# Hybrid attention layer: score banks, look-ahead and small work in the differential heads

## The chip, the cores and the metric

The kernel runs on one core of one Trainium2 chip. The metric is the device time of one execution in microseconds (us). In the profile PE is TensorE (PEld its weight loads), DVE is VectorE, ACT is ScalarE, POOL is GpSimd, and SP is the queue that issues nearly all DMAs. L12 is line 12 of the kernel before; lines of the changed kernel are named as such.

## The reference

One decoder layer over 2048 tokens of width 1024. A pre-normed projection feeds eight stick-breaking heads of 64 and four differential heads (two 64-wide query and key maps each, values of 128). One output projection and a SwiGLU FFN follow. The change is in the differential heads:

```python
for start in range(0, S, Q_BLOCK):                      # S = 2048, Q_BLOCK = 128
    end = start + Q_BLOCK
    s = einsum('bhcqd,bhckd->bhcqk', q[:, :, :, start:end], k[:, :, :, :end]) * scale
    causal = arange(end)[None, :] <= arange(start, end)[:, None]
    p = softmax(where(causal, s, -inf), axis=-1)
    a = p[:, :, 0] - lam * p[:, :, 1]
    outs.append(einsum('bhqk,bhkd->bhqd', a, v[:, :, :end]))
```

Each head's output is RMS-normed afterwards. Queries and keys are normed and rotated (rope) before.

## The kernel before

The work is staged: norm and transposes of x; groups g = 0 to 3, pairs of stick-breaking heads; groups 4 to 7, one differential head each; the second part of the output projection; the FFN. Numbers are kept as a high and a low 16-bit half, so most products are three matmuls.

**Units.** A differential head has 16 query tiles i of 128 queries, with L = 128 (i + 1) columns of scores. `unit_diff` (L887) handles one map m and one chunk j of at most 1024 columns, so a tile has two units up to i = 7 and four from i = 8 on (n = 2 chunks), in the order m = 1, then m = 0. A head has 48 units. A unit has three parts:

- `scores` (L893): score matmuls into a place in PSUM, two per 512 columns, and the mask on the diagonal.
- `front` (L908): VectorE takes the row maximum of the scores (the helper `big`, so the trace shows L178), and for the second chunk joins it to the first one's (L919).
- `main` (L921): ScalarE makes the bias from the joined maximum (L925, only for chunk 0) and the exponential into SBUF with its row sum (L931). A two-chunk tile's first exponential thus needs both chunks' maxima.

**Clock.** Units are issued one by one. `clock.at(d, fn)` puts follow-up work d units later. After the last unit of a tile come `coefs` (sums joined at L950, reciprocal L951, factor L952), per chunk `mix` (VectorE, p0 + c p1), `high` (a float16 copy, on ScalarE at L974 for two chunks, on VectorE at L976 for one, then a DMA transpose at L327), `low` (the rest, L985 on GpSimd or VectorE through `big`), then `values` (matmuls with the transposed halves), `copy` (L1009, L1011), `power`, `store_high` (L1024), `store` (L1029). The transposed halves lie in a ring of eight.

**The loop** (from L1233) does for unit n: due evacuations; the maxima of unit n + 1; due small work; `main` of n; further due work; `look_ahead(n)`, which issues scores up to unit n + 2; then projection work (`fill_next`) as long as TensorE's count of columns is behind a goal. Since every engine takes its instructions in order, this order is the schedule. PSUM has eight banks of 512 columns; in the differential heads banks 0 to 5 are three fixed places of 1024 columns for scores, whatever a unit's width, and the last two serve projections and values (`places`, `place`).

**Projection.** `project_diff` (L593) makes q, k and v of 512 tokens as fill: `evac_v` (L641) writes v's halves on VectorE (L643, L644), twice in each of the 16 projections; `high` (L698) casts the rotated q on VectorE (L703) and k on ScalarE (L704).

Of the kernel before, what the change touches and what calls it, by code (L numbers as in the profile page):

```python
# [12 lines left out]
ALU = mybir.AluOpType  # L13
# [51 lines left out]
def hybrid_layer_kernel(  # L65
# [159 lines left out]
    with ExitStack() as actx:  # L225
# [28 lines left out]


# [343 lines left out]
        def project_diff(c, g):  # L599
# [19 lines left out]
            for j in range(4):  # L619
                yield from bank_totals()  # L620
                ps = pj_tile("pj")
                part(j, 0, ps[:, 0:128])
                yield
                part(j, 1, ps[:, 128:256])

                def evac(j=j, ps=ps):
                    nc.scalar.activation(
                        st[:, :, j], ps.rearrange("p (t m d) -> p t m d", t=2, m=2),
                        AF.Copy, scale=OUT_SC)

                clock.at(1, evac, "mid")
                yield END
                if j % 2 == 0:
                    continue
                yield from bank_totals()
                ps = pj_tile("pj").rearrange("p (j n) -> p j n", j=2)
                part(j - 1, 2, ps[:, 0])
                yield
                part(j, 2, ps[:, 1])

                def evac_v(j=j, ps=ps):  # L641
                    vh, vl = v[:, j - 1:j + 1, 0, :], v[:, j - 1:j + 1, 1, :]
                    nc.vector.tensor_scalar(vh, ps, OUT_SC, None, ALU.mult)  # L643
                    nc.vector.scalar_tensor_tensor(vl, ps, OUT_SC, vh, ALU.mult, ALU.subtract)  # L644

                clock.at(1, evac_v, "mid")
                yield END
# [51 lines left out]
            def high():  # L699
                n2 = r["rt"].bitcast(F16)  # L700
                r["n"] = n2[:, 0:1024], n2[:, 1024:2048]
                r["nk"], r["nq"] = (halves(a) for a in r["n"])
                nc.vector.tensor_copy(r["nq"][:, :, :, 0, :], xq)  # L703
                nc.scalar.copy(r["nk"][:, :, :, 0, :], xk)  # L704
# [56 lines left out]
        def unit_sb(g, s, c, a, cx, step):  # L761
# [114 lines left out]
            return scores, None, main, W, 3 * W + 3 * W + (384 if diag else 0)  # L876
# [9 lines left out]
        def unit_diff(g, i, m, j, cx):  # L886
# [6 lines left out]
            def scores():  # L893
# [3 lines left out]
                z = u["z"] = place("z", 1024)  # L897
# [10 lines left out]
            def front():  # L908

                if m == 1 and j == 0:  # L910
                    cx["mx"] = small("mx", 4, bufs=3)
                    cx["nb"] = small("nb", 4, bufs=3)
                    cx["su"] = small("su", 4, bufs=3)
                    cx["cf"] = small("cf", 4, bufs=8)
                mx = cx["mx"]
                jj = 2 * j + m
                big(nc.vector.reduce_max, mx[:, jj:jj + 1], u["z"][:, 0:e - b], axis=AX.X)
                if j > 0:
                    nc.vector.tensor_max(mx[:, m:m + 1], mx[:, jj:jj + 1], mx[:, m:m + 1])  # L919

            def main():  # L921
                mx, nb, su = cx["mx"], cx["nb"], cx["su"]
                jj = 2 * j + m
                if j == 0:
                    nc.scalar.activation(nb[:, m:m + 1], mx[:, m:m + 1], AF.Identity,  # L925
                                         scale=nds_sc, bias=lnk)
# [7 lines left out]
                if m == 0 and j == n - 1:  # L934
# [5 lines left out]
                    clock.at(7 + n, values, "mid")  # L940
                    clock.at(8 + n, copy, "")
                    clock.at(9 + n, power)
                    clock.at(10 + n, store_high, "hi")
                    clock.at(11 + n, store, "")

            def coefs():
                su, cf = cx["su"], cx["cf"]
                steps = []
                if n == 2:
                    steps.append(lambda: nc.vector.tensor_add(su[:, 0:2], su[:, 0:2], su[:, 2:4]))  # L950
                steps += [lambda: nc.vector.reciprocal(cf[:, 0:1], su[:, 1:2]),  # L951
                          lambda: nc.vector.tensor_scalar(cf[:, 1:2], cf[:, 0:1], su[:, 0:1], nlam,  # L952
                                                          ALU.mult, ALU.mult)]

                def eps():
                    nc.gpsimd.tensor_scalar(cf[:, 2:3], su[:, 0:1], su[:, 0:1], scl[g][:, 2:3],
                                            ALU.mult, ALU.mult)
# [10 lines left out]
            def high(jc):  # L968
# [4 lines left out]
                if n == 2:  # L973
                    nc.scalar.copy(wh, p0)  # L974
                else:
                    nc.vector.tensor_copy(wh, p0)  # L976
# [49 lines left out]
            def store():  # L1026
# [8 lines left out]
                2 * (e - b) + (3 * L if m == 0 and j == n - 1 else 0))  # L1035
# [158 lines left out]
        for g in range(NG):  # L1194
# [7 lines left out]
            for n, (scores, front, main, w, _) in enumerate(us):  # L1202
                done += w
                plan.append((g, scores, front, main, work * min(1, done / tot),
                             PROJ * min(1, max(0, n - 2) / 11 if g == NG - 1 else (n + 1) / first)))
# [27 lines left out]
        for n, (g, scores, front, main, goal, due) in enumerate(plan):  # L1233
# [6 lines left out]
            if front is not None and (n == 0 or plan[n - 1][0] != g):  # L1240
                front()
            if n + 1 < len(plan) and plan[n + 1][0] == g and plan[n + 1][2] is not None:
                plan[n + 1][2]()
# [6 lines left out]
            look_ahead(n)  # L1250
            if g == NG - 1 and since == 18:
# [519 lines left out]
```

## Time and profile before

| | |
|---|---|
| median of 3 runs | 2860.58 us (2860.14 to 2867.91) |
| the profiled execution | 2863.87 us, its span 2862.1 us |
| mean granted TensorE clock | 0.955 |
| exponentials of the differential heads (L931) | 192, from 753.8 to 1425.0 us |

The page gives the busy time of each engine over the span, then groups of instructions by line, with count, busy time, mean time of one and the idle time just before them with what ended it. A view by windows gives the busy time of each engine in chosen stretches; the view of waits adds up who waited for whom. "psum" is the one tile that holds all of PSUM.

### The profile page before, as it was taken

To read this page: it belongs to the slowest core of one execution; us is meant where nothing else is said; L and a number is where in the kernel's file an instruction comes from. 1 tells how busy PE (TensorE), PEld (TensorE's weight loads), DVE (VectorE), ACT (ScalarE), POOL (GpSimd) and SP (SyncE) were. 2 spreads that over 40 slices of the span, in tenths; PEclk is the share of its full clock that TensorE was granted. 3 is DMA by queue.
4 is the path that set the end of the run, shared out by engine and by line. 5 is a ranking of instruction groups with operands and counts; after the bars stand their busy time and mean duration, and the time that the engine had idled before them with its cause. 6 is when DMAs were issued, how large, how long until landed. Compare 5 with 4: busy or idle time off the path is not lost.

```text
span 2862.1 us, 50497 instructions
## 1 busy us (share of the span) xinstructions
PE 2532.1 (88%) x19626; PEld 1466.2 (51%) x19626; DVE 2325.4 (81%) x3609; ACT 1513.6 (53%) x2523; POOL 1463.8 (51%) x1131
## 2 busy tenths in 40 slices
PE   6978888887786887877997998999999999999999
PEld 4534445455675676665853444444444444444444
DVE  7898999888888888998739689989777767776776
ACT  5778788876555655555515444444443433343332
POOL 2454545547667676674214656655444444444442
PEclk8989999998898998988999999999999999999999
DMA  4576877866554555667766221221217421112111
GB/s 160 93 144 120 144 140 139 139 130 122 103 93 89 99 104 105 130 123 165 172 169 140 89 100 67 81 78 60 89 45 148 155 96 45 45 44 89 45 45 74
DMA packets 734096, 301.49 MB, mean 105 GB/s; under 512 B 618656, under 2 KB 713120, under 8 KB 733856
## 3 DMA queue, kind: packets, MB, share of 16 engines
q1 hardware_dynamic: 733712, 298.23, 46.3%
q8 instruction: 153, 2.51, 0.4%
q14 instruction: 87, 0.71, 0.1%
q0 software_dynamic: 144, 0.03, 0.0%
HBM read 127.27 MB, written 28.31 MB: 54 GB/s over the span
## 4 chain that ended last, share of the span: by engine, by line
PE 44%; DVE 20%; POOL 6%; issue 5%; ACT 5%; DMA 4%; SPq 1%; DVEq 0%; POOLq 0%; ACTq 0%
PE pw L167 34%; PE psum L167 10%; DVE fs L1379 2%; DMA wt<-wh 2%; DVE acc_a L1636 2%; DVE mx L178 2%; DVE pp L178 1%; DVE hh L1423 1%; DVE pp L807 1%; DVE wh L836 1%; DMA q<-rt 1%; DVE wmx L105 1%; DVE rt L683 1%; POOL sc L1553 1%; POOL qss L108 1%
## 5 line engine op out<-in xcount | busy, mean ns | idle before, releaser
L167 PE MATMUL pw<-t,fs 128*128 128x512 f16 x3696 | 808.3, 381 | 17.2 <-issue 11.7
L167 PEld LDWEIGHTS <-fs 128*128 128x128 f16 x3696 | 360.6, 98 | 455.9 <-issue 18.4
L818 POOL TENSOR_TENSOR pp<-pp 128x1024 f32<-128x1024 f32 (+1 forms) x160 | 325.0, 2031 | 319.4 <-DVE pp L815 141.2
L167 PE MATMUL pw<-acc_b,at 128*128 128x512 f16 x2112 | 463.3, 379 | 18.1 <-DVE cg L1561 11.7
L167 PE MATMUL psum<-k,q 64*128 64x512 f16 (+4 forms) x1600 | 288.6, 378 | 161.3 <-ACT pp L931 80.8
L167 PE MATMUL psum<-ws,h_hi 128*128 128x128 f16 x4096 | 380.2, 225 | 20.1 <-ACT psum L1011 10.6
L167 PE MATMUL psum<-ws,h_lo 128*128 128x128 f16 x2048 | 369.2, 225 | 0.0
L167 PEld LDWEIGHTS <-h_hi 128*128 128x128 f16 x4096 | 329.9, 101 | 49.2 <-issue 37.7
L167 PEld LDWEIGHTS <-at 128*128 128x128 f16 x2112 | 205.6, 98 | 267.8 <-issue 22.6
L1564 POOL TENSOR_TENSOR cg<-cg,cu 128x512 f32<-128x512 f32 x88 | 112.4, 1278 | 371.4 <-ACT cg L1563 337.3
L1636 DVE SCALAR_TENSOR_TENSOR acc_a<-pw,isd,acc_a 128x512 f32<-128x512 f32 x352 | 248.9, 744 | 54.5 <-PE pw L167 54.1
L1378 ACT ACTIVATE fs<-acc_b,fst 128x512 f16<-128x512 f32 x264 | 176.1, 714 | 216.6 <-POOL acc_b L1367 143.3
L1379 DVE SCALAR_TENSOR_TENSOR fs<-acc_b,fst,fs 128x512 f16<-128x512 f32 x264 | 248.6, 982 | 31.6 <-ACT fs L1378 31.5
L1553 POOL TENSOR_TENSOR sc<-sc 128x512 f32<-128x512 f32 x132 | 220.0, 1682 | 91.3 <-ACT sc L1547 91.3
L807 DVE TENSOR_TENSOR_SCAN pp<-pp,psum 128x256 f32<-128x256 f32 (+1 forms) x320 | 195.8, 652 | 58.7 <-ACT psum L804 57.8
L167 PEld LDWEIGHTS <-q 64*128 64x128 f16 (+1 forms) x1600 | 94.9, 99 | 271.7 <-issue 114.3
L1547 ACT COPY sc<-pw 128x512 f32<-128x512 f32 x176 | 100.3, 581 | 217.6 <-PE pw L167 191.3
L167 PEld LDWEIGHTS <-h_lo 128*128 128x128 f16 x2048 | 207.3, 101 | 0.0
L836 DVE TENSOR_TENSOR wh<-pp,wh 128x1024 f16<-128x1024 f32 (+1 forms) x160 | 205.0, 1281 | 1.1 <-DMA wt<-wh 1.1
L931 ACT ACTIVATE pp<-psum,nb,ds_sc 128x1024 f32<-128x1024 f32 (+4 forms) x192 | 183.0, 954 | 21.8 <-DVE pp L178 8.5
L178 DVE TENSOR_REDUCE mx<-psum 128x1 f32<-128x1024 f32 (+4 forms) x192 | 173.6, 905 | 19.9 <-PE psum L167 19.1
L802 ACT ACTIVATE pp<-psum,gsc 128x1024 f32<-128x1024 f32 (+1 forms) x160 | 164.8, 1030 | 38.2 <-PE psum L167 34.4
(215 smaller groups left out, 4503.6 us busy)
## 6 DMA issues: line engine op xcount, KB each, us to landing
acc_b<-in_w_gate_dram SPq DMA_DIRECT2D x22, 1024.0 KB, 5.3
acc_b<-in_w_up_dram SPq DMA_DIRECT2D x22, 1024.0 KB, 7.6
acc_b<-in_w_down_dram SPq DMA_DIRECT2D x22, 1024.0 KB, 9.5
raw<-in_w_in_dram SPq DMA_DIRECT2D x24, 512.0 KB, 4.5
pp<-in_x_dram SPq DMA_DIRECT2D x16, 512.0 KB, 5.2
wt<-wh SPq DMA_TRANSPOSE x512, 3.2
raw<-in_w_o_dram SPq DMA_DIRECT2D x16, 512.0 KB, 4.1
mt<-mix_d SPq DMA_DIRECT2D x32, 256.0 KB, 3.1
```

The source lines that it names most:

```text
L167: nc.tensor.matmul(ps, lhsT=lhsT, rhs=rhs, start=start, stop=stop)
L178: fn(*a, **k)
L802: nc.scalar.activation(be, z[:, :, 0:W], AF.Sigmoid, scale=sc[:, 0:1])
L807: nc.vector.tensor_tensor_scan(ga, ga, z[:, h, P:W][:, ::-1], 2.0 ** 14 if diag else cx[a][:, h, 0:1], ALU.mult, ALU.mult)
L818: nc.gpsimd.tensor_mul(b4, b4, gp[:, :, 1:P + 1].rearrange("p h (r n) -> p h r n", r=1).to_broadcast([128, 2, 2, P]))
L836: nc.vector.tensor_sub(wl[:, 0:n], b2, u["wh"][:, 0:n])
L931: nc.scalar.activation(pt, u["z"][:, 0:e - b], AF.Exp, scale=ds_sc, bias=nb[:, m:m + 1], accum_out=su[:, jj:jj + 1])
L1378: nc.scalar.activation(w[:, m, 0:4], src, AF.Copy, scale=sw)
L1379: nc.vector.scalar_tensor_tensor(w[:, m, 4:8], src, sw, w[:, m, 0:4], ALU.mult, ALU.subtract)
L1553: nc.gpsimd.tensor_add(s[m], s[m], y[m])
L1564: nc.gpsimd.tensor_mul(g, g, u)
L1636: nc.vector.scalar_tensor_tensor(acc[:, i, hs], ps, pr.isd, acc[:, i, hs], ALU.mult, ALU.add)
```

## The change

1. **Banks.** In the differential heads a unit takes one bank if it is at most 512 columns wide, else two neighbouring ones, of the six (`take_banks`), and gives them back after its own `look_ahead` (`give_banks`). `look_ahead` issues scores up to unit n + 3 while banks are free.
2. **Maxima.** In unit n all maxima up to unit n + 2 are taken whose scores have been issued.
3. **Values.** `values` and all behind it come one unit later, but for the last tile of a head.
4. **Small work.** `evac_v` goes through `halved` (high half on ScalarE, low half on VectorE); q's cast goes to ScalarE; `high` casts on ScalarE for one-chunk tiles too; the joins of maxima and sums are a `tensor_reduce` over two elements instead of an in-place `tensor_max` and `tensor_add`. The small tiles mx, nb and su become parts of one tile with five buffers, which the trace of the changed kernel will call mx.

```diff
+        def banks_for(w):
+            free = [o is None for o in owner]
+            if w > 512:
+                at = [b for b in range(5) if free[b] and free[b + 1]]
+                return min(at, key=lambda b: max(had[b], had[b + 1]), default=None)
+            at = [b for b in range(6) if free[b]]
+            return min(at, key=lambda b: (free[b ^ 1], had[b]), default=None)
...
+        def give_banks(n):
+            for b in range(6):
+                if owner[b] == n:
+                    owner[b], had[b] = None, n
...
                 def evac_v(j=j, ps=ps):
-                    vh, vl = v[:, j - 1:j + 1, 0, :], v[:, j - 1:j + 1, 1, :]
-                    nc.vector.tensor_scalar(vh, ps, OUT_SC, None, ALU.mult)
-                    nc.vector.scalar_tensor_tensor(vl, ps, OUT_SC, vh, ALU.mult, ALU.subtract)
+                    halved(ps, v[:, j - 1:j + 1, 0, :], v[:, j - 1:j + 1, 1, :])
...
-                nc.vector.tensor_copy(r["nq"][:, :, :, 0, :], xq)
+                nc.scalar.copy(r["nq"][:, :, :, 0, :], xq)
...
-                z = u["z"] = place("z", 1024)
+                z = u["z"] = take_banks(ahead[0], e - b)
...
                 if j > 0:
-                    nc.vector.tensor_max(mx[:, m:m + 1], mx[:, jj:jj + 1], mx[:, m:m + 1])
+                    nc.vector.tensor_reduce(mx[:, 4 + m:5 + m], mx[:, m:4:2], axis=AX.X,
+                                            op=ALU.max)
...
-                    clock.at(7 + n, values, "mid")
-                    clock.at(8 + n, copy, "")
-                    clock.at(9 + n, power)
-                    clock.at(10 + n, store_high, "hi")
-                    clock.at(11 + n, store, "")
+                    d = n if i == NT - 1 else n + 1
+                    clock.at(7 + d, values, "mid")
+                    clock.at(8 + d, copy, "")
+                    clock.at(9 + d, power)
+                    clock.at(10 + d, store_high, "hi")
+                    clock.at(11 + d, store, "")
...
                 if n == 2:
-                    steps.append(lambda: nc.vector.tensor_add(su[:, 0:2], su[:, 0:2], su[:, 2:4]))
+                    steps.append(lambda: nc.vector.tensor_reduce(
+                        su[:, 4:6], su[:, 0:4].rearrange("p (j m) -> p m j", m=2), axis=AX.X,
+                        op=ALU.add))
...
-                if n == 2:
-                    nc.scalar.copy(wh, p0)
-                else:
-                    nc.vector.tensor_copy(wh, p0)
+                nc.scalar.copy(wh, p0)
...
-                if ahead[0] > n + (1 if g < SBP else 2):
+                if mode[0] == "diff":
+                    if ahead[0] > n + 3 or banks_for(plan[ahead[0]][6]) is None:
+                        break
+                elif ahead[0] > n + (1 if g < SBP else 2):
                     break
...
-            if n + 1 < len(plan) and plan[n + 1][0] == g and plan[n + 1][2] is not None:
-                plan[n + 1][2]()
+            seen = max(seen, n)
+            while seen < min(ahead[0], n + 3) and plan[seen][0] == g and plan[seen][2] is not None:
+                plan[seen][2]()
+                seen += 1
...
             look_ahead(n)
+            give_banks(n)
```

The order of VectorE before, in the second differential head: pp_129<-pp_125 of 128 columns is the mix of tile 8's second chunk, mx_12548 holds the maxima of tile 10, whose first chunk has 1024 and second 384 columns.

```order
L178 SCALAR_TENSOR_TENSOR pp_129<-pp_125,cf_12142,pp_129 128x128
L643 TENSOR_SCALAR v_12175<-psum_107 128x2x128
L644 SCALAR_TENSOR_TENSOR v_12175<-psum_107,v_12175 128x2x128
L178 TENSOR_REDUCE mx_12548<-psum_107 128x1
L1029 SCALAR_TENSOR_TENSOR mxs_12518<-on_12388,oss_12390,mxs_12518 128x128
L178 SCALAR_TENSOR_TENSOR pp_123<-pp_127,cf_12142,pp_123 128x1024
L178 TENSOR_REDUCE mx_12548<-psum_107 128x1
L950 TENSOR_TENSOR su_12353<-su_12353 128x2
L919 TENSOR_TENSOR mx_12548<-mx_12548 128x1
```

The same place now, with tile 10's maxima in mx_12428:

```order
L573 SCALAR_TENSOR_TENSOR v_12109<-psum_107,v_12109 128x2x128
L178 TENSOR_REDUCE mx_12428<-psum_107 128x1
L145 TENSOR_SCALAR wsw_12318<-wsw_12318 128x1
L1058 SCALAR_TENSOR_TENSOR mxs_12421<-on_12302,oss_12304,mxs_12421 128x128
L709 TENSOR_TENSOR rt_12201<-st_11407,cs_12198 128x8x32
L710 TENSOR_TENSOR st_11407<-st_11407,cs_12198 128x8x32
L147 TENSOR_SCALAR gsc_122<-wsw_12318 128x1
L148 RECIPROCAL wsw_12318<-gsc_122 128x1
L178 SCALAR_TENSOR_TENSOR pp_129<-pp_125,cf_12085,pp_129 128x128
L178 TENSOR_REDUCE mx_12428<-psum_107 128x1
L944 TENSOR_REDUCE mx_12428<-mx_12428 128x1
```

Tile 10's first maximum stands ahead of the mix instead of behind it, one unit earlier, and of v only the low half is left on VectorE. ScalarE before, over the exponentials of tile 10's other map, that is units of 1024 and 384 columns:

```order
L925 ACTIVATE nb_12549<-mx_12548,lnk_118,nds_sc_121 128x1
L931 ACTIVATE pp_123,su_12550<-psum_107,nb_12549,ds_sc_120 128x1024
L1024 ACTIVATE mxs_12716<-on_12616,oss_12618 128x128
L931 ACTIVATE pp_128,su_12550<-psum_107,nb_12549,ds_sc_120 128x384
L974 CAST wh_132<-pp_125 128x256
```

and now:

```order
L952 ACTIVATE mx_12428<-mx_12428,lnk_118,nds_sc_121 128x1
L957 ACTIVATE pp_123,mx_12428<-psum_107,mx_12428,ds_sc_120 128x1024
L957 ACTIVATE pp_128,mx_12428<-psum_107,mx_12428,ds_sc_120 128x384
L572 ACTIVATE v_12109<-psum_107 128x2x128
L1053 ACTIVATE mxs_12728<-on_12635,oss_12637 128x128
```

The high half of v (L572) has come into ScalarE's queue, behind two exponentials, and the store (L1024, now L1053) is one unit later.

More of the change, by code (lines that the diff above doesn't have):

```diff
@@ L253, in place, with take_banks @@
             return psum[:, ps[n]:ps[n] + w]
+        owner, had = [None] * 6, [-1] * 6
+        def banks_for(w):
[5 more added lines that the diff above has]
+            return min(at, key=lambda b: (free[b ^ 1], had[b]), default=None)
+        def take_banks(n, w):
+            if mode[0] == "diff":
+                b, m = banks_for(w), (w + 511) // 512
+                z = psum[:, b * 512:b * 512 + w]
+            else:
+                z = place("z", 1024)
+                b, m = places[mode[0]]["z"][turn["z"]] // 512, 2
+            owner[b:b + m] = [n] * m
+            return z
+        def give_banks(n):
+            for b in range(6):
+                if owner[b] == n:
+                    owner[b], had[b] = None, n
         ident = onp.tile([128, 128], F32, tag="on", name="ident")
@@ L874, in store @@
                 clock.at(1, lambda: store_mix(g, s * 256, 256, st))
-            return scores, None, main, W, 3 * W + 3 * W + (384 if diag else 0)
+            return scores, None, main, W, 3 * W + 3 * W + (384 if diag else 0), 1024
         def units_diff(g):
@@ L910, in front @@
                 if m == 1 and j == 0:
[L911 to L914, printed above, removed]
+                    t = small("mx", 14, bufs=5)
+                    cx["mx"], cx["nb"], cx["su"] = t[:, 0:6], t[:, 6:8], t[:, 8:14]
+                    cx["cf"] = small("cf", 4, bufs=9)
                 mx = cx["mx"]
@@ L924, in main @@
                 if j == 0:
-                    nc.scalar.activation(nb[:, m:m + 1], mx[:, m:m + 1], AF.Identity,
-                                         scale=nds_sc, bias=lnk)
+                    top = mx[:, m:m + 1] if n == 1 else mx[:, 4 + m:5 + m]
+                    nc.scalar.activation(nb[:, m:m + 1], top, AF.Identity, scale=nds_sc, bias=lnk)
                 while gps:
@@ L1034, in unit_diff @@
             return scores, front, main, (e - b) + (0.35 * L if m == 0 and j == n - 1 else 0), (
-                2 * (e - b) + (3 * L if m == 0 and j == n - 1 else 0))
+                2 * (e - b) + (3 * L if m == 0 and j == n - 1 else 0)), e - b
         def own(g):
@@ L1201, in hybrid_layer_kernel @@
             done = 0.0
-            for n, (scores, front, main, w, _) in enumerate(us):
+            for n, (scores, front, main, w, _, cols) in enumerate(us):
                 done += w
                 plan.append((g, scores, front, main, work * min(1, done / tot),
-                             PROJ * min(1, max(0, n - 2) / 11 if g == NG - 1 else (n + 1) / first)))
+                             PROJ * min(1, max(0, n - 2) / 11 if g == NG - 1 else (n + 1) / first),
+                             cols))
             fills[g] = filler(g)
@@ L1221, in look_ahead @@
                 g = plan[ahead[0]][0]
-                if ahead[0] > n + (1 if g < SBP else 2):
+                if mode[0] == "diff":
+                    if ahead[0] > n + 3 or banks_for(plan[ahead[0]][6]) is None:
+                        break
+                elif ahead[0] > n + (1 if g < SBP else 2):
                     break
@@ L1232, in hybrid_layer_kernel @@
         since = 0
-        for n, (g, scores, front, main, goal, due) in enumerate(plan):
+        seen = 0
+        for n, (g, scores, front, main, goal, due, _) in enumerate(plan):
             if g != g0:
@@ L1239, in hybrid_layer_kernel @@
             clock.run("ev")
-            if front is not None and (n == 0 or plan[n - 1][0] != g):
-                front()
-            if n + 1 < len(plan) and plan[n + 1][0] == g and plan[n + 1][2] is not None:
-                plan[n + 1][2]()
+            seen = max(seen, n)
+            while seen < min(ahead[0], n + 3) and plan[seen][0] == g and plan[seen][2] is not None:
+                plan[seen][2]()
+                seen += 1
             for kind in ("", "main", "mid", None):
```

8 lines of the change are left out of this document (5 added, 3 removed).

## The prediction, as made before the change was run

> **What bounds the kernel now.** I read the page first, its span and the busy times of the engines:
>
> ```profile
> span 2862.1 us, 50497 instructions
> PE 2532.1 (88%) x19626; PEld 1466.2 (51%) x19626; DVE 2325.4 (81%) x3609; ACT 1513.6 (53%) x2523; POOL 1463.8 (51%) x1131
> ```
>
> TensorE (PE) has the largest share, but this is a mean over stages, so the busy times by stretch come next (us busy, instructions in brackets, then the granted clock):
>
> ```profile
> core 0: us, PE busy (x) PEld busy (x) DVE busy (x) ACT busy (x) POOL busy (x), PEclk, DMA share, GB/s
> 80.00:750.00 670.00, 555.13 (x5688) 333.84 (x5684) 595.96 (x1018) 532.62 (x742) 357.30 (x187) 0.92 0.72 131
> 753.00:1425.00 672.00, 533.74 (x6589) 448.86 (x6589) 586.54 (x1005) 371.79 (x896) 414.08 (x412) 0.92 0.61 118
> 1465.00:2862.00 1397.00, 1351.67 (x6559) 613.63 (x6557) 1067.43 (x1459) 558.23 (x805) 669.00 (x486) 0.99 0.27 83
> ```
>
> The last stretch, FFN and output product, is TensorE's (1351.7 of 1397 us), and the change does not reach it. The differential heads are the 672 us from 753 on: VectorE (DVE) is busy for 87%, TensorE for 79%, ScalarE (ACT) for 55%. Each head goes through four kinds of query tiles: i = 0 to 3 (one chunk of at most 512 columns), 4 to 7 (one chunk of 640 to 1024), 8 to 11 (1024 and at most 512), 12 to 15 (1024 and over 512). The next rows cut at these borders: tiles 4 to 7 of the four heads are the 1st, 2nd, 4th and 7th, the 3rd to 6th are the third head whole, the last is tiles 12 to 15 of the last head.
>
> ```profile
> 776.30:801.70 25.40, 23.51 (x327) 19.59 (x325) 22.65 (x44) 14.96 (x42) 8.42 (x14) 1.00 0.65 108
> 952.60:973.80 21.20, 20.37 (x274) 17.04 (x273) 18.91 (x40) 15.41 (x45) 6.44 (x12) 0.98 0.32 66
> 1089.40:1115.30 25.90, 21.03 (x283) 18.37 (x282) 23.23 (x39) 13.68 (x40) 24.90 (x23) 0.90 0.61 105
> 1115.30:1137.70 22.40, 19.16 (x240) 15.43 (x238) 19.13 (x38) 15.43 (x44) 8.28 (x15) 0.95 0.53 95
> 1137.70:1193.60 55.90, 43.22 (x580) 37.21 (x579) 48.29 (x82) 28.29 (x75) 34.23 (x34) 0.94 0.70 142
> 1193.60:1254.10 60.50, 49.05 (x673) 42.04 (x670) 59.71 (x92) 35.25 (x74) 44.51 (x42) 0.92 0.57 114
> 1282.20:1307.50 25.30, 16.14 (x202) 12.40 (x199) 22.60 (x42) 16.47 (x45) 9.49 (x15) 0.95 0.62 125
> 1367.50:1426.40 58.90, 58.56 (x562) 48.63 (x561) 44.18 (x79) 30.02 (x62) 13.09 (x16) 1.00 0.75 169
> ```
>
> In tiles 12 to 15 of the third head VectorE works 59.7 of 60.5 us: nothing else sets the pace there. In tiles 4 to 7 of three heads TensorE is nearly full (23.5 of 25.4, 20.4 of 21.2, 19.2 of 22.4), and in the last row wholly (58.56 of 58.90). In between, VectorE leads with a few us of waiting. The waits over 750 to 1425 say who waits for whom (us, times, longest):
>
> ```profile
> PE psum L167 <- ACT pp L931: 80.8, 55, 5.6
> PE psum L167 <- DMA wt<-wh: 22.4, 18, 4.3
> DVE mx L178 <- PE psum L167: 19.1, 22, 4.0
> DVE mxs L1029 <- ACT mxs L1024: 9.1, 10, 3.6
> ```
>
> It is a ring: score matmuls wait for an exponential to empty their banks, maxima wait for scores, and the exponential waits for maxima (below). VectorE has the least slack in it, so its work counts most.
>
> **Part by part: VectorE's work.** The groups that are moved or replaced, in the same stretch (count | us busy, mean ns):
>
> ```profile
> L643 DVE TENSOR_SCALAR v<-psum 128x256 f16<-128x256 f32 x26 | 10.7, 413 | 1.5 <-PE psum L167 1.4
> L703 DVE CAST rt<-st 128x512 f16<-128x512 f32 x14 | 8.6, 615 | 0.0
> L976 DVE CAST wh<-pp 128x128 f16<-128x128 f32 (+7 forms) x32 | 18.3, 571 | 3.9 <-issue 3.9
> L919 DVE TENSOR_TENSOR mx<-mx 128x1 f32<-128x1 f32 x64 | 19.9, 312 | 0.9
> L950 DVE TENSOR_TENSOR su<-su 128x2 f32<-128x2 f32 x31 | 9.1, 292 | 0.0
> ```
>
> The first three go to ScalarE: 10.7 + 8.6 + 18.3 = 37.6 us. The last two become reductions over two elements. Their nearest row is a reduction of 128x2 in the stage before:
>
> ```profile
> L815 DVE TENSOR_REDUCE pp<-pp x96: 140/146/155, 103.7 to 751.7; 128x2 f32<-128x2 f32 x96
> ```
>
> Its longest is 155 ns, so I take 147: 64 x (312 - 147) + 31 x (292 - 147) = 10.6 + 4.5 = 15.1 us; the other end is no saving, if whatever lengthens L919 lengthens its successor. The Trainium skill, SBUF — State Buffer, § Who interferes with whom, says that on this chip a tensor_reduce never contends with GpSimd, while an instruction with two SBUF inputs does. By that rule the 15.1 us stand whole, without it between 0 and 15.1; no row here shows such a reduction beside this stage's GpSimd work, and the narrow 140 to 155 ns of L815 agree.
>
> Together 52.7 us of VectorE's 586.5. Not all of it comes out at the end. In the three stretches of tiles 4 to 7 where TensorE is full I count it at nothing: tiles 4 to 7 hold 3328 of the 4608 columns of L976, so 13.2 of its 18.3 us, three quarters of that is 9.9; of L643 and L703 a share of 69/672, 2.0. In the last row, TensorE's own, go 8 maxima and 4 sums at 165 and 145 ns, 1.9. That leaves 52.7 - 13.8 = 39 us. (The six L643 and two L703 before 753 lie beside a ScalarE that is itself 80% busy; counted at nothing.)
>
> **What ScalarE gets.** It copies the same shapes in these times:
>
> ```profile
> L627 ACT ACTIVATE st<-psum 128x256 f32<-128x256 f32 x52 | 19.5, 376 | 21.4 <-DMA q<-st 16.8 <-PE psum L167 4.5
> L704 ACT CAST rt<-st 128x512 f16<-128x512 f32 x14 | 8.6, 617 | 17.8 <-POOL st L687 17.8
> L925 ACT ACTIVATE nb<-mx,lnk,nds_sc 128x1 f32<-128x1 f32 x128 | 49.0, 383 | 138.2 <-DVE mx L919 116.1 <-DVE mx L178 21.9
> L931 ACT ACTIVATE pp<-psum,nb,ds_sc 128x1024 f32<-128x1024 f32 (+7 forms) x191 | 181.8, 952 | 21.8 <-DVE pp L178 8.5 <-POOL wh L985 5.4 <-DVE wh L178 1.4
> ```
>
> 26 x 376 + 14 x 617 = 18.4 us, and for L976 about as much as on VectorE (615 and 617 ns for the same 128x512 cast), some 20: 38 us on an engine that idles 300 of 672 and waits 138 us for maxima at L925. It is hidden there. The Trainium skill, Perfetto Trace Analysis, § Optimizing Scalar/DVE Operations, speaks against the move unless VectorE is saturated: in a performance mode it is the faster of the two. By the two means here the casts cost the same; where VectorE isn't saturated, in tiles 4 to 7, the sum has no gain either way.
>
> **A new wait.** evac_v now writes the high half on ScalarE and the low half on VectorE in the same step (L572 and L573 of the changed kernel). ScalarE has the exponential ahead of it in its queue, and everything behind the low half on VectorE, the next maximum first, waits too. The nearest row is the same pair in the stick-breaking stage (48 pairs):
>
> ```profile
> L545 DVE SCALAR_TENSOR_TENSOR v<-psum,v x16: 672/680/693, 57.8 to 626.2; 128x512 f16<-128x512 f32 x16
> ...
>   ACT v L544: 7.5, 3
>   ACT k L544: 7.3, 3
>   ACT q L544: 5.9, 5
> ```
>
> 20.7 us over 48 pairs is 0.43 us each, there with ScalarE 80% busy. The ends are 0 and a whole exponential with its bias and the copy, 383 + 952 + 376 ns = 1.7 us. I take 0.2 us, half of the row, since ScalarE has half again the slack: 26 x 0.2 = 5 us lost.
>
> **Scores and maxima ahead, values later.** Counting six banks over the units of a head: one-bank tiles (i = 0 to 3) and the mixed ones (8 to 11) get a third unit ahead, two-bank tiles (4 to 7, 12 to 15) keep two, since three of them fill six banks. So half of the units are served, and in the saturated tiles 12 to 15 nothing moves. In the served ones VectorE idles 25.9 - 23.2 = 2.7 and 55.9 - 48.3 = 7.6 us in the third head; over four heads 41 us, as an estimate. The earlier maxima free ScalarE from L925, the earlier exponential frees the banks for which TensorE waits 80.8 us; values one unit later meet transposes that have landed (22.4 us). Of all this only what VectorE waited for counts at the end: between 0 and 41, and I take a quarter, 10. The values keep their transposed halves a unit longer; there are eight, a tile uses four in four units, and the first is taken again two units after its release, so SP's queue has nothing new to wait for.
>
> Sum: 39 + 10 - 5 = 44 us less. The profiled execution took 2863.87 us, 1.8 more than its span; the median of the three runs is 2860.58, and I take the 44 from that: 2817.
>
> **Rivals.** (a) *ScalarE holds up VectorE at evac_v: slower.* If nearly every one of the 32 pairs waits for the whole exponential, 32 x 1.7 = 54 us, and if the moved 38 us also delay the exponentials so that the look-ahead brings nothing, it is 39 - 54: 15 slower, 2876. It decides from 39/32 = 1.2 us per pair on. For it: in tiles 12 to 15 ScalarE still gets its maximum just before, so the exponential really stands ahead of the copy. Against it: the 0.43 us, and VectorE has mixes of over 1 us to do in between. (b) *The ring is bound by its latency, not by VectorE.* Then 37.6 us change sides and come back as 38 on ScalarE, and only the shorter small steps (15.1 - 1.9) remain: 2847. For it: 138 us at L925 and 81 of TensorE behind the exponential. Against it: 59.7 of 60.5. (c) *More than forecast.* If look-ahead lifts VectorE's share from 87 to 90%, the stretch is (586.5 - 52.7)/0.90 = 593 instead of 672: 2782. Against it: TensorE's 534 us would then be 90% busy too, and it cannot give up the 59 us of the last row. (d) *The third unit ahead is seldom granted.* Then the 10 fall away: 2827; the order of the changed kernel shows the earlier maxima, so this is small.
>
> **How the numbers follow.** Forecast 0.58, (a) 0.08, (b) 0.14, (c) 0.13, (d) 0.07. About 0.3%, 8.6 us, is what a measurement of this kernel can tell from no change. The forecast, (c), (d) and nearly two thirds of (b), which lies 13 us below, are faster: 0.86; the rest of (b) and a little of (a) are the same, 0.07; slower 0.07. The range runs from 2786, where the 52.7 us come out whole with half of the 41 (just short of (c)), to 2850, which holds (b) and leaves out (a).
>
> **What would show it.** Right: between 753 and the end of the heads VectorE's busy time falls by some 50 us, the stretch by about 44, and its share stays near 87%; the groups at L976, L703 and L643 are gone, and the reductions at the new L944 and L979 take about 150 ns; the wait of L573 for L572 is about 5 us; L925's wait shrinks in tiles 0 to 3 and 8 to 11, and not in 12 to 15. Wrong: a wait at L573 above 30 us (a); VectorE's busy time down but the stretch as long, with idle before its maxima (b); reductions that take over 300 ns.

## The result: slower

The change makes the kernel 0.6% slower: 2881.77 us median of four runs (2875.42 to 2884.37), the kernel before beside it 2863.80 (2860.14 to 2867.91); ratio 1.0062, 95% interval 1.005 to 1.0074, so 14 to 21 us. The forecast was 2817, its range 2786 to 2850.

The profiled execution of the changed kernel took 2884.37 us. Its page begins:

```profile
span 2882.6 us, 50442 instructions
...
PE 2547.6 (88%) x19626; PEld 1476.5 (51%) x19626; DVE 2286.2 (79%) x3529; ACT 1547.9 (54%) x2603; POOL 1455.2 (50%) x1131
```

VectorE lost 39.2 us of busy time and ScalarE gained 34.3, as intended, and the span grew by 20.5. By stretch (us busy, then granted clock), the changed kernel; the second row runs from the first exponential of the differential heads to the last:

```profile
core 0: us, PE busy (x) PEld busy (x) DVE busy (x) ACT busy (x) POOL busy (x), PEclk, DMA share, GB/s
80.00:753.00 673.00, 559.13 (x5690) 337.15 (x5689) 591.25 (x1009) 534.44 (x749) 356.36 (x187) 0.91 0.73 131
757.90:1441.10 683.20, 542.95 (x6603) 456.32 (x6603) 554.19 (x935) 404.08 (x971) 406.63 (x412) 0.90 0.61 115
1480.00:2882.00 1402.00, 1358.26 (x6572) 615.92 (x6570) 1068.47 (x1459) 557.89 (x805) 669.03 (x486) 0.99 0.28 83
```

The same stretch of the kernel before, first to last exponential:

```profile
753.80:1426.20 672.40, 534.94 (x6600) 449.93 (x6600) 587.74 (x1006) 372.20 (x897) 413.28 (x412) 0.92 0.61 118
```

VectorE is busy 33.6 us less, and the stretch is 10.8 us longer; its share fell from 87 to 81%, where the forecast wanted it unchanged. From exponential to exponential, the four heads' tiles 12 to 15 got 11.9 us longer and tiles 8 to 11 2.7, while tiles 0 to 3 got 3.6 shorter; so the loss lies mostly in tiles 12 to 15, from which (in the third head) the forecast took VectorE to set the pace, though VectorE is busy 7.5 us less in them. TensorE does the same matmuls in 8.0 us more, at a clock of 0.90 instead of 0.92. (Of the other 10 us of the span, 4 lie ahead of the heads and 6 behind; one profile of each kernel can't say what they are worth.) The new and some changed groups in the heads of the changed kernel, count | busy, mean ns | idle before:

```profile
L1058 DVE SCALAR_TENSOR_TENSOR mxs<-on,oss,mxs 128x128 f16<-128x128 f32 x60 | 38.3, 638 | 18.0 <-ACT mxs L1053 17.7
...
L573 DVE SCALAR_TENSOR_TENSOR v<-psum,v 128x256 f16<-128x256 f32 x26 | 10.9, 420 | 16.1 <-ACT v L572 16.1
...
L944 DVE TENSOR_REDUCE mx<-mx 128x1 f32<-128x2 f32 x64 | 9.8, 153 | 1.0
...
L979 DVE TENSOR_REDUCE mx<-mx 128x2 f32<-128x4 f32 x31 | 4.5, 145 | 2.6 <-ACT pp L957 2.6
```

The moved groups (37.6 us) and the shorter joins (14.7) are 52.3 us of work that left VectorE, but its busy time fell by 33.6, because other groups take longer. The store's last step is one of them, 638 ns above and 542 in the kernel before:

```profile
L1029 DVE SCALAR_TENSOR_TENSOR mxs<-on,oss,mxs 128x128 f16<-128x128 f32 x60 | 32.5, 542 | 9.9 <-ACT mxs L1024 9.1 <-issue 0.6
```

The waits in the heads of the changed kernel (us, times, longest):

```profile
PE psum L167 <- ACT pp L957: 100.5, 47, 6.9
...
ACT on L1038 <- PE psum L167: 75.4, 28, 6.3
...
ACT mx L952 <- DVE mx L944: 47.7, 22, 4.5
...
ACT mxs L1053 <- DMA mix_d<-mxs: 22.0, 8, 5.9
...
PE psum L167 <- DMA wt<-wh: 10.1, 10, 2.8
```

Beside them, of the kernel before:

```profile
ACT on L1009 <- PE psum L167: 42.9, 24, 3.3
...
PE psum L167 <- DMA wt<-wh: 21.5, 17, 4.3
...
ACT mxs L1024 <- DMA mix_d<-mxs: 1.3, 1, 1.3
```

So the early maxima and the late values seem to do what they were meant to do: the bias waits 47.7 instead of 116.1 us for a joined maximum, TensorE half as long for transposed weights. (Part of the first is a wait that changed its place: ScalarE's copy, in the same queue, waits 75.4 instead of 42.9.) But TensorE, which all this should feed, waits 100.5 us for exponentials instead of 80.8.

### The profile page after: what moved, and what is told of

Its sections match the earlier page's. It is cut to its first block, busy times and chain, and to the rows that moved or that the text cites. A ratio compares the mean times of both kernels' runs of the same rounds, so it can differ in the third digit from the quotient of the medians.

```text
span 2882.6 us, 50442 instructions
## 1 busy us (share of the span) xinstructions
PE 2547.6 (88%) x19626; PEld 1476.5 (51%) x19626; DVE 2286.2 (79%) x3529; ACT 1547.9 (54%) x2603; POOL 1455.2 (50%) x1131
## 4 chain that ended last, share of the span: by engine, by line
PE 45%; DVE 18%; POOL 7%; ACT 5%; issue 5%; DMA 5%; SPq 0%; DVEq 0%; POOLq 0%; ACTq 0%
PE pw L167 34%; PE psum L167 11%; DMA wt<-wh 2%; DVE fs L1415 2%; DVE acc_a L1672 2%; DVE mx L178 1%; DVE hh L1459 1%; DVE pp L833 1%; POOL qss L108 1%; DVE wh L862 1%; POOL wh L1014 1%; DVE pp L178 1%; DMA raw<-in_w_o_dram 1%; DVE wmx L105 1%; POOL sc L1589 1%
## 5 line engine op out<-in xcount | busy, mean ns | idle before, releaser
L167 PE MATMUL pw<-acc_b,at 128*128 128x512 f16 x2112 | 464.7, 380 | 16.8 <-DVE cg L1597 11.5
L167 PE MATMUL psum<-k,q 64*128 64x512 f16 (+4 forms) x1600 | 295.2, 382 | 184.0 <-ACT pp L957 100.5
L167 PE MATMUL psum<-ws,h_hi 128*128 128x128 f16 x4096 | 391.2, 228 | 18.6 <-ACT psum L1040 11.0
L167 PE MATMUL psum<-ws,h_lo 128*128 128x128 f16 x2048 | 379.2, 228 | 0.0
L167 PEld LDWEIGHTS <-h_hi 128*128 128x128 f16 x4096 | 336.9, 103 | 46.1 <-issue 36.6
L957 ACT ACTIVATE pp<-psum,mx,ds_sc 128x1024 f32<-128x1024 f32 (+4 forms) x192 | 183.2, 954 | 31.8 <-DVE pp L178 17.7
L178 DVE TENSOR_REDUCE mx<-psum 128x1 f32<-128x1024 f32 (+4 forms) x192 | 173.1, 905 | 25.8 <-PE psum L167 22.8
L828 ACT ACTIVATE pp<-psum,gsc 128x1024 f32<-128x1024 f32 (+1 forms) x160 | 164.8, 1030 | 37.6 <-PE psum L167 34.3
```

Of the source, the lines that this page charges most:

```text
L167: nc.tensor.matmul(ps, lhsT=lhsT, rhs=rhs, start=start, stop=stop)
L178: fn(*a, **k)
L828: nc.scalar.activation(be, z[:, :, 0:W], AF.Sigmoid, scale=sc[:, 0:1])
L957: nc.scalar.activation(pt, u["z"][:, 0:e - b], AF.Exp, scale=ds_sc, bias=nb[:, m:m + 1], accum_out=su[:, jj:jj + 1])
```

## The experiments

no_values and after_copy_later are the changed kernel with the edit shown; all others are the kernel before with a part of the change or with the edit shown. Ratios are to the kernel before, run beside them. Microseconds by which a kernel is called faster or slower are the ratio's, of 2863. The stretch, VectorE's busy time and TensorE's gaps (times in which it neither multiplies nor loads weights for over 3 us: count, sum) are those of the heads in one profile of each, worked out from the starts and ends in its trace; that profile can lie some 6 us off the median.

| kernel | ratio (95%) | heads, us | VectorE busy | gaps over 3 us |
|---|---|---|---|---|
| before | 1 | 672.4 | 587.7 | 8, 33.0 |
| the change | 1.0062 (1.0050 to 1.0074) | 683.2 | 554.2 | 13, 57.5 |
| values_only | 1.0062 (1.0048 to 1.0076) | 684.3 | 588.0 | 16, 62.9 |
| no_values | 1.0058 (1.0044 to 1.0071) | 684.8 | 548.2 | 14, 56.9 |
| small_only | 1.0013 (1.0004 to 1.0022) | 674.1 | 556.0 | 8, 34.7 |
| ahead_only | 1.0040 (1.0027 to 1.0053) | 678.2 | 589.9 | 14, 58.6 |
| cast_only | 0.9998 (0.9989 to 1.0007) | 670.2 | 576.6 | 8, 33.4 |
| moves_only | 1.0022 (1.0011 to 1.0033) | 675.8 | 572.5 | 7, 28.6 |
| joins_only | 0.9995 (0.9985 to 1.0004) | 672.9 | 584.3 | 10, 41.3 |
| v_half_only | 1.0026 (1.0015 to 1.0037) | 682.4 | 582.2 | 7, 30.0 |
| q_cast_only | 1.0014 (1.0005 to 1.0022) | 677.9 | 580.0 | 7, 28.7 |
| values_one_chunk | 0.9999 (0.9990 to 1.0009) | 670.8 | 585.5 | 12, 49.9 |
| values_two_chunks | 1.0055 (1.0042 to 1.0068) | 685.2 | 592.4 | 12, 49.1 |
| values_behind | 1.0062 (1.0050 to 1.0074) | 687.4 | 592.3 | 11, 44.4 |
| copy_later | 1.0076 (1.0062 to 1.0090) | 689.6 | 584.0 | 10, 51.1 |
| values_copy_later | 1.0144 (1.0125 to 1.0163) | 706.4 | 586.2 | 14, 68.4 |
| after_copy_later | 1.0064 (1.0049 to 1.0078) | 685.4 | 553.3 | 16, 73.2 |
| values_early | 1.0216 (1.0201 to 1.0232) | 729.8 | 576.3 | 19, 79.4 |
| cast_joins | 0.9998 (0.9989 to 1.0008) | 670.0 | 573.9 | 6, 25.8 |
| low_on_vector | 0.9984 (0.9975 to 0.9992) | 662.3 | 581.7 | 9, 34.2 |

### Which part costs

values_only takes part 3 of the change alone, no_values leaves it out, small_only takes part 4 alone, ahead_only parts 1 and 2 (with the joint small tile, which they need).

```diff
 values_only, to the kernel before
-                    clock.at(7 + n, values, "mid")
+                    d = n if i == NT - 1 else n + 1
+                    clock.at(7 + d, values, "mid")
...
 no_values, to the changed kernel
-                    d = n if i == NT - 1 else n + 1
+                    d = n
```

> The kernel before with values and what follows one unit later, nothing else. Values theory (the later values stand ahead of other scores on TensorE, and ScalarE's copy of their result, ahead of the next exponential, waits longer; that is what the change lost): 10 to 20 us slower than before. ScalarE theory (the work moved to ScalarE holds up the exponentials and VectorE's low halves; that is what the change lost): within 5 us of before. Ring theory (the ring of scores, maxima and exponentials is bound by its latency, so no part matters much alone): within 5 us of before.

> The changed kernel with values back at their old unit. Values theory: 15 to 30 us faster than the change, that is 0 to 15 us faster than before. ScalarE theory: still 10 to 20 us slower than before. Ring theory: within 5 us of before.

> The kernel before with the small work moved to ScalarE and the joins as reductions of two elements, nothing else. ScalarE theory: 10 to 20 us slower than before. Values theory: 10 to 40 us faster than before, since 40 to 50 us of work leave VectorE. Ring theory: 0 to 13 us faster (only the shorter joins count).

> The kernel before with the banks counted, scores up to three and maxima up to two units ahead, nothing else (VectorE keeps its work). Ring theory: 5 to 20 us faster than before, since the ring gets slack. Values theory and ScalarE theory: 0 to 10 us faster than before.

Each part alone is slower: values 17.8 us, look-ahead 11.5, small work 3.7. They don't add up: 33 us in sum, 17.8 together, and beside the other parts the late values cost next to nothing (no_values is 16.6 slower, the whole 17.8). The values theory holds for the part alone and falls for the whole, which is no faster without it. The ScalarE theory has no_values right and falls with small_only (3.7 instead of 10 to 20) and values_only. The ring theory falls with values_only, and none of the three had ahead_only slower. In ahead_only the bias's wait for joined maxima falls from 116.1 to 78.7 us, and part of it comes back one step on, where the exponential takes its weight tile:

```profile
ACT mx L953 <- DVE mx L946: 78.7, 32, 5.7
...
ACT pp L958 <- DVE pp L178: 15.2, 16, 2.3
...
ACT pp L958 <- POOL wh L1015: 14.0, 7, 2.6
```

Before, these last two are 8.5 and 5.4 us (in the prediction's row of L931). That is 15 of the 37 us; where the rest went this doesn't show.

### The small work, piece by piece

cast_only moves the one-chunk cast to ScalarE, moves_only the half of v and the cast of q, joins_only has the joins as reductions.

```diff
 cast_only
-                if n == 2:
-                    nc.scalar.copy(wh, p0)
-                else:
-                    nc.vector.tensor_copy(wh, p0)
+                nc.scalar.copy(wh, p0)
 moves_only (v_half_only: the first, q_cast_only: the second)
+                    halved(ps, v[:, j - 1:j + 1, 0, :], v[:, j - 1:j + 1, 1, :])
...
+                nc.scalar.copy(r["nq"][:, :, :, 0, :], xq)
 joins_only (and the same for the sums)
+                    nc.vector.tensor_reduce(mx[:, 4 + m:5 + m], mx[:, m:4:2], axis=AX.X,
+                                            op=ALU.max)
```

> The kernel before, with one edit: the high half of a weight tile of one chunk is cast on ScalarE instead of VectorE (18.3 us of VectorE's work in the heads). All the small work together left the heads 1.7 us longer: 8 us lost in the one-chunk tiles 0 to 7, 6 us gained in tiles 8 to 15. Cast theory (the cast stands in ScalarE's row ahead of the next exponential, which then starts later, and TensorE gets its psum later): slower by 5 to 12 us, all of it in tiles 0 to 7. VectorE theory (the forecast's: the work that leaves VectorE counts): faster by 8 to 18 us. Ring theory (each step waits in turn, neither engine's load counts): within 4 us.

> The kernel before, with the two other moves to ScalarE alone: the first half of v and the cast of q (10.7 and 8.6 us of VectorE's work in the heads), joins and the one-chunk cast as before. Cast theory (only the one-chunk cast hurts, the rest of the small work helps): faster by 3 to 8 us. VectorE theory: faster by 8 to 19 us. Ring theory: within 4 us.

> The kernel before, with the joins of two chunks as reductions over two columns, nothing else: about 12 to 15 us of VectorE's work in tiles 8 to 15 is gone, no engine gets more work and nothing changes its place. VectorE theory: faster by 8 to 15 us, since VectorE is the engine with the least slack there. Ring theory: faster by 0 to 5 us, the two chains that a join stands in being shorter by 0.2 us each, 64 times. Cast theory says nothing against either.

The cast theory falls: that cast costs nothing (0.6 us faster, 3.1 faster to 2.0 slower). The joins bring 1.4 us, not clear of zero. moves_only is 6.3 us slower, which no theory had; so its two halves were taken apart:

> The kernel before, with the first half of v made by ScalarE instead of VectorE, nothing else (10.7 us leave VectorE). Together with the cast of q it made the run 6.4 us slower. Evacuation theory (VectorE's second half now waits for ScalarE, whose row holds an exponential ahead of it; VectorE stands still there with its maxima behind, 0.2 us to 3 us each): slower by 3 to 8 us, most of it in tiles 4 to 7, where TensorE's projections use the same psum. VectorE theory of the forecast: faster by 5 to 10 us.

> The kernel before, with the cast of q on ScalarE instead of VectorE, nothing else (8.6 us leave VectorE). Evacuation theory: within 3 us of before, since nothing on VectorE waits for this cast. Cast-of-q theory (the rival here: the cast waits for GpSimd's rotation on ScalarE's row, with exponentials behind it): slower by 3 to 8 us. VectorE theory of the forecast: faster by 4 to 8 us.

The half of v costs 7.4 us though it takes 10.7 from VectorE; 7.3 of the profile's 10.0 us lie in tiles 4 to 7, as the evacuation theory said. Its wait in v_half_only:

```profile
DVE v L545 <- ACT v L544: 14.3, 11, 1.9
```

VectorE stands still there for longer than the work that it gave away. The cast of q costs 4.0 us (1.4 to 6.3), nearer to its own theory; what through stays open.

### Late values: two theories that fell

```diff
 values_one_chunk
+                    d = n + 1 if n == 1 else n
 values_two_chunks
+                    d = n + 1 if n == 2 and i < NT - 1 else n
 values_behind: as values_two_chunks, the late values held until the scores are issued
             look_ahead(n)
+            while held:
+                held.pop(0)()
```

> The kernel before, with values, copy, power and stores one unit later in tiles 0 to 7 only (one chunk), as before in tiles 8 to 15. With all tiles a unit later the run was 18 us slower: 10.2 us lost in tiles 8 to 11, 3.6 in tiles 12 to 15, 3.5 gained in tiles 0 to 3, 1.4 lost in tiles 4 to 7. Step theory (the loss is that in a tile of two chunks a shift by one unit puts the values ahead of the scores that the next exponential needs, while before they stood ahead of scores needed a unit later): within 5 us of before. Queue theory (values that come later keep buffers and the copy waiting everywhere): slower by 5 us or more, in tiles 0 to 7.

> The kernel before, with values, copy, power and stores one unit later in tiles 8 to 14 only (two chunks), as before in the others. One unit later in tiles 0 to 7 changed the time by 0.4 us, in all tiles by 18. Step theory (in a tile of two chunks the shift puts the values directly ahead of the last scores of the next half, on whose maximum the next exponential waits): slower by 12 to 20 us. If the two parts do not add (a ring that loses only when every tile is late): within 6 us.

> As the kernel with values a unit later in the tiles of two chunks, but TensorE is given the values behind the scores of that unit instead of ahead of them (tiles 8 to 13; tile 14 as there). Step theory: most of the loss is gone, within 6 us of before, and the wait of ScalarE's bias for the maxima is back to its value before. Queue theory (the loss comes of what hangs on late values: the copy waiting on ScalarE's row for values, buffers kept longer): as slow as the kernel with values later in those tiles, or slower, since the copy comes one unit after the values in both and now has less time.

Late values cost only where they belong to tiles of two chunks (15.8 us; 0 for the others), as the step theory said. But its reason is not borne out: with the values behind the scores the kernel is as slow, as the queue theory said. (It isn't ruled out either, since in values_behind the copy has less time behind the values, and its longer wait can hide a gain.) What these kernels have in common is a longer wait of ScalarE's copy, 72.0 us in values_two_chunks and 97.5 in values_behind against 42.9. So the copy got more time:

```diff
 copy_later (values_copy_later on top of values_two_chunks, after_copy_later of the change)
-                    clock.at(8 + n, copy, "")
+                    clock.at(9 + n, copy, "")
                     ... power, store_high and store one later too
```

> The kernel before, with copy, power and the stores one unit later and the values where they were. The copy of before waits 42.9 us for TensorE in the heads with ScalarE's next exponential queued behind it. Copy theory (this wait is what late values make longer, and exponentials and then TensorE pay for it): faster by 3 to 12 us, the copy's wait for TensorE under 15 us. Place theory (the place of the values in TensorE's row, and the rings that they hold, cost the time, the copy's wait is only a sign of it): within 3 us of before.

> The kernel with values one unit later in the tiles of two chunks (14 us slower than before, its copy waits 72 us for TensorE), with copy, power and stores one more unit later in all tiles. Copy theory: within 5 us of before, the copy's wait under 25 us. Place theory: still slower by 9 us or more.

> The whole change (18 us slower than before, its copy waits 75 us for TensorE), with copy, power and stores one more unit later in all tiles. Copy theory: the 11 us of the values go, 3 to 8 us slower than before. Place theory: still slower by 14 us or more.

The copy theory falls outright: instead of 3 to 12 us faster, copy_later is 21.8 slower, and with late values in the two-chunk tiles it is 41, about the sum of the two costs (37.6). The place theory doesn't explain copy_later either (it had no change). A later copy makes waits of its own, by the waits of copy_later:

```profile
ACT on L1009 <- PE psum L167: 58.7, 21, 6.3
PE psum L167 <- ACT psum L1011: 31.9, 10, 9.2
...
ACT mxs L1024 <- DMA mix_d<-mxs: 22.2, 5, 7.6
```

TensorE now waits 31.9 us (18.7 before) for the square that follows the copy, and ScalarE 22.2 (1.3) for the output buffer. And why the copy's wait misled can be read in values_two_chunks:

```profile
ACT nb L925 <- DVE mx L919: 92.0, 47, 4.0
...
ACT on L1010 <- PE psum L167: 72.0, 29, 5.6
```

The copy waits 29.1 us more, but the bias behind it in ScalarE's row 24.1 less (18.9 with the bias's second row, 23.8 against 18.6): ScalarE would have stood still there for the maximum anyway, in the main. In after_copy_later the copy's wait is 38.7 us, and the time is that of the change. What late values cost the two-chunk tiles through is not settled.

Is any lateness bad, then? values_early takes a unit away.

```diff
 values_early
+                    d = n - 1
```

> The kernel before, with values, copy, power and stores one unit earlier in all tiles. One unit later cost 18 us. Lateness theory (each unit by which a tile's end comes later costs, by the buffers and rows that it holds up): faster by 5 to 18 us. Two-sided theory (before stands at the best place: earlier, TensorE waits for the transposed weights, whose wait is 51.3 us in the heads before, and the values stand in its row ahead of scores): slower by 5 us or more, that wait over 75 us.

It is 62 us slower, and the waits bear out the two-sided theory:

```profile
ACT on L1010 <- PE psum L167: 155.2, 41, 9.9
PEld L167 <- DMA wt<-wh: 105.6, 52, 7.1
...
PE psum L167 <- DMA wt<-wh: 94.8, 47, 6.9
```

TensorE waits 200 us for transposed weights against 51.5. Of the three distances that of the kernel before is the best.

### Does VectorE's load set the time at all?

cast_joins puts the two free pieces together; low_on_vector goes the other way and gives VectorE the subtraction that GpSimd did.

```diff
 low_on_vector, to cast_joins
-                if jc == 0 and n == 2:
-                    nc.gpsimd.tensor_sub(wl, p0, wh)
-                else:
-                    big(nc.vector.tensor_sub, wl, p0, wh)
+                big(nc.vector.tensor_sub, wl, p0, wh)
```

> The kernel before, with the one-chunk cast on ScalarE and the joins as reductions: the two parts of the change that cost nothing alone (ratios 0.9998 and 0.9995); some 30 us leave VectorE. Ring theory (VectorE's load in the heads doesn't set the time): within 4 us of before. VectorE theory of the forecast: faster by 15 to 25 us.

> The kernel with the one-chunk cast on ScalarE and the joins as reductions (some 15 us of VectorE's time in the heads gone, 0.1% from before), and in addition the low half of the first chunk in tiles 8 to 15 made by VectorE instead of GpSimd: 31 subtractions of 128x1024 that took GpSimd 2182 ns each (67.6 us) and take VectorE an estimated 1.1 to 1.7 us each (34 to 54 us). VectorE theory of the forecast: slower by 15 to 40 us, all in tiles 8 to 15. GpSimd theory (the chain of work goes through these subtractions for 15 us, and they hold up VectorE's other work beside them): faster by 5 to 15 us. Ring theory (neither engine's load sets the time): within 4 us.

The heads of cast_joins, then of low_on_vector:

```profile
752.70:1422.70 670.00, 538.38 (x6600) 450.81 (x6600) 573.91 (x974) 389.85 (x930) 411.34 (x412) 0.91 0.61 118
```

```profile
752.80:1415.10 662.30, 529.48 (x6600) 442.74 (x6600) 581.65 (x1004) 389.73 (x930) 359.97 (x382) 0.93 0.63 120
```

14 us less on VectorE bring nothing (0.6 us faster, 3.1 faster to 2.3 slower), where the forecast's theory wanted 15 to 25. Thirty large subtractions more on it, and the kernel is 4.6 us faster than before (2.3 to 7.2), in the profile with 10 us less in the heads: the only kernel here that is faster than before beyond its interval. The forecast's theory, 15 to 40 us slower, falls; between the GpSimd theory (5 to 15 faster) and the ring theory (within 4) the run doesn't decide sharply. It is a weaker test of VectorE's load than it looks, though: beside cast_joins VectorE's busy time rose by only 7.7 us, and it is still 6.1 below that of the kernel before. The subtractions cost it 1416 ns each, its share of the group here in low_on_vector:

```profile
L178 DVE TENSOR_TENSOR wh<-pp,wh 128x1024 f16<-128x1024 f32 x37 | 52.4, 1416 | 0.2 <-ACT wh L978 0.2
```

In the kernel before VectorE did seven of that shape, and GpSimd the others, in two groups:

```profile
L178 DVE TENSOR_TENSOR wh<-pp,wh 128x1024 f16<-128x1024 f32 x7 | 12.1, 1726 | 0.0
```

```profile
L985 POOL TENSOR_TENSOR wh<-pp,wh 128x1024 f16<-128x1024 f32 x30 | 64.7, 2157 | 84.4 <-ACT wh L974 83.7 <-POOL qss L108 0.6
```

40 us more in that one group and 7.7 in all: the rest of VectorE's work got shorter beside a GpSimd that is busy 360 us instead of 411. In the mean the cast of q takes 464 ns instead of 702 in cast_joins (615 before) and the mixes 1084 instead of 1167, which is no less than before (1072). That GpSimd's work lengthens VectorE's is argued from these times; it was not tried alone. The Trainium skill, Perfetto Trace Analysis, § Optimizing GPSIMD Operations, says to prefer other engines for an operation where one can; 2157 against 1416 ns, and this run, agree.

## Why the prediction was wrong

**The step that failed** is the first: "VectorE has the least slack in it, so its work counts most", from 59.7 of 60.5 us busy, and with it the 39 of 52.7 us that were counted at the end. In cast_joins VectorE is busy 13.8 us less, and 0.6 us come out at the end; in small_only it is busy 31.7 us less, and the kernel is 3.7 us slower (1.1 to 6.3), the wait for the half of v included. A busy engine is not yet the path. The chain of waits, followed back through the heads of the kernel before, gave a hint of that; its sum by line:

```profile
by line: PE psum L167 23.7%; issue 9.9%; DVE mx L178 7.3%; DVE pp L178 5.6%; DMA wt<-wh 3.1%; DMA q<-rt 2.9%; POOL qss L108 2.6%; POOL wh L985 2.3%; DVE rt L683 2.2%; DVE wh L178 2.1%; POOL cf L956 1.9%; DMA q<-st 1.8%; POOL oss L108 1.8%; 
```

All pieces added up by engine, it runs through VectorE for 211 of the 672 us, the largest part but under a third, through TensorE for 159, GpSimd 111, DMA 72, ScalarE 31. And in the changed kernel:

```profile
by line: PE psum L167 26.5%; issue 10.1%; DVE mx L178 5.6%; DMA wt<-wh 4.7%; POOL qss L108 3.7%; POOL wh L1014 3.2%; DVE pp L178 3.1%; DMA raw<-in_w_o_dram 3.0%; ACT pp L957 1.9%; DMA q<-st 1.8%; POOL st L711 1.8%; POOL st L713 1.8%; DVE st
```

Its VectorE part fell by 62 us, to 150, more than the work removed. TensorE's rose by 22, GpSimd's by 33, ScalarE's by 15, DMA's by 8: another engine's step was next late at once. These sums are rough, since in values_only, where VectorE keeps all its work, its part is 236. Which parts lose by themselves is shown (look-ahead, late values, the half of v, the cast of q); through which waits they lose stays open, but for the half of v.

**The reductions** were sized rightly: 153 and 145 ns against 147, so 64 x (312 - 153) + 31 x (292 - 145) = 14.7 us against 15.1. The rule from the Trainium skill (SBUF — State Buffer, § Who interferes with whom) that a tensor_reduce is not held up by GpSimd holds here: beside a GpSimd that is busy for 60% of the heads none of the 64 at L944 takes over 156 ns. They are worth 1.4 us at the end (4.3 gained to 1.1 lost), a tenth of their count. One reason can be read: in joins_only VectorE's busy time in the heads falls by 3.4 us only (the table), as its mixes take longer. Here before, then in joins_only:

```profile
L178 DVE SCALAR_TENSOR_TENSOR pp<-pp,cf 128x128 f32<-128x128 f32 (+7 forms) x94 | 100.6, 1072 | 0.0
```

```profile
L178 DVE SCALAR_TENSOR_TENSOR pp<-pp,cf 128x128 f32<-128x128 f32 (+7 forms) x94 | 108.0, 1151 | 0.0
```

So half of the 14.7 us came back in that group. What lengthens the mixes isn't shown.

**ScalarE's 38 us "hidden"** holds for the one-chunk cast (0), not for the cast of q (4.0 us). The Trainium skill (Perfetto Trace Analysis, § Optimizing Scalar/DVE Operations) says that moving work to ScalarE may make sense where VectorE is saturated. At 59.7 of 60.5 us it looked so, and yet none of the moves brought anything.

**The new wait** was 16.1 us over 26 pairs, 0.62 each and not 0.2, within its bounds and far below rival (a)'s 1.2 and the 30 us that would have proved it. In v_half_only it is 14.3 us, and the half of v is a loss by itself (7.4 us). Rival (a)'s sign and number (2876) came out near by luck; its mechanism didn't, since ahead_only and values_only lose without any such wait.

**Scores and maxima ahead**: in ahead_only the wait shrank where it was said to, from 16.8 to 11.0 us in tiles 0 to 3, 39.4 to 2.6 in 8 to 11, and in 12 to 15 not (76.7 and 76.1; both rows of the bias together, each bias counted to its own tile). In the whole change it is 19.0, 1.9 and 45.8; the fall in tiles 12 to 15, which the forecast excluded, comes with late values alone too (51.4 in values_only). What failed is its worth: a gain of 10 us forecast, a loss of 11.5 measured. Rival (b), a ring bound by its latency, is nearest in kind, but it still had 13 us of gain, and took earlier scores and maxima to be harmless.

**Values later** was counted only as a help to TensorE. That help came (51.5 to 22.0 us of wait for transposes, both rows), and the part alone costs 17.8 us. That "SP's queue has nothing new to wait for" looked at the queue alone and left out copy and store_high on ScalarE, whose waits grew (42.9 to 75.4 us for the values, 1.3 to 22.0 for the output buffer). Whether these waits are what costs the time isn't shown.

## What to carry to other kernels

Where engines take turns in a ring, an engine that is busy for 87% of a stage, even for 59.7 of 60.5 us, need not set its pace: look up how much of the chain of waits runs through it, and try a cheap kernel that changes little but its load, as cast_joins does, before moving more. Read its busy time again afterwards, since work taken off it can come back as longer work beside it (52.3 us taken off, 33.6 less busy). A wait that shrinks is worth only what the next one doesn't take back, and a wait that grows may stand in the place of another: add up an engine's waits in a row before blaming one. Work that is timed by hand against a DMA can lose on both sides of its distance (here 62 us one unit earlier, 18 one unit later).

## What the runs showed of the hardware

After a long idle time TensorE starts slowly. In the changed kernel, in order of time (start, us, what, idle before):

```profile
900.82 1.02 PE L167 MATMUL psum<-k,q 128*128 128x512 f16 x4 [0.37 <-ACT pp L957]
907.94 1.87 PE L167 MATMUL psum<-k,q 128*128 128x512 f16 x4 [6.10 <-ACT pp L957]
...
909.71 1.91 PE L167 MATMUL psum<-k,q 128*128 128x512 f16 x4
...
913.89 1.03 PE L167 MATMUL psum<-k,q 128*128 128x512 f16 x4
```

The same four matmuls take 1.02 us, after 6.1 us of idle 1.87 and 1.91, and some 6 us after the start 1.03 again. Over the heads of the changed kernel projection matmuls start 89 ns apart in the 4 us after a gap of over 3 us (mean of 76 pairs), 77 after one of 1 to 3 us (191) and 57 otherwise. The Trainium skill, TensorE: Matmul & The Clock Gate, § Part 1: The HAM clock gate, tells of such a gate with a window of about 3.4 us; the rows agree. So a long gap costs more than its own length. TensorE idles about as long in the heads of the changed kernel as in those of the kernel before (140.2 and 137.5 us), but in 13 gaps of over 3 us instead of 8, and its same matmuls take 8.0 of the 10.8 us that the stretch got longer. In ahead_only there are 14 such gaps, the clock is 0.90 instead of 0.92, and TensorE is busy 7.8 us longer in a stretch that is 5.8 us longer. In the slowest kernel, values_early, there are 19 such gaps, and the clock is 0.88:

```profile
753.00:1482.80 729.80, 557.64 (x6627) 462.87 (x6627) 576.28 (x1009) 370.08 (x898) 402.89 (x412) 0.88 0.57 109
```

It is no rule for the whole table: values_one_chunk has 12 such gaps and loses nothing, v_half_only 7 and loses 7.4 us. That the gaps cause the change's loss was not tried by itself.
